# Gate and up of one layer as seven block products instead of eight, and its down products in four sections instead of three

## The chip, the core and the metric

The kernel runs on one core of a Trainium2 chip. The metric is the device time of one execution in microseconds (us), the median of several runs. The core has five engines with queues of their own: TensorE (PE, matrix products; its weight loads are PEld), VectorE (DVE), ScalarE (ACT), GpSimd (POOL) and SyncE (SP, which here issues nearly all DMAs). They meet only through semaphores. SBUF is the on-chip memory with 128 partitions, PSUM the eight banks into which TensorE writes.

## The reference

Two layers of a hybrid encoder over 512 prompt tokens and 64 sample tokens (576 in all, D_MODEL 1024, D_FF 2816). Each layer is a token mixer (a state-space scan and a windowed attention), then a feed-forward block. What the change touches is the feed-forward block of the second layer:

```
h2 = rmsnorm(x, norm_ffn_g) * (1 + sc_f) + sh_f          # [576, 1024]
gate, up = jnp.split(h2 @ w_gate_up, 2, axis=-1)          # w_gate_up [1024, 2 * 2816]
x = x + gt_f * ((jax.nn.silu(gate) * up) @ w_down)        # w_down [2816, 1024]
```

## The kernel before

Activations lie transposed: channels on the partitions, the 576 tokens along the row, in two halves of 288 (`H0`, `H1`; `HALF` = 288). Every fp32 product is made of three fp32r products: an operand is split into a rounded part (`hi`) and the rest (`lo`), and TensorE adds hi*hi, lo*hi and hi*lo in PSUM. `split` does this with one ScalarE cast (`S.copy` into `whi`) and one subtraction (`wlo`) on VectorE or, where the granule's `eng` is `G`, on GpSimd.

Weights come in granules (`Gran`) of 8 x 128 rows by 128 columns, 512 KB, through a ring of four raw buffers (`RAWB`). A granule becomes two `whi` and two `wlo` tiles of [128, 4, 128], in rings of four each (`WB`). `loads` issues the DMA of the next granule once an earlier one has been split; `advance` splits the granules of the present job, and after the job's first half one granule more. A `Job` is 128 output columns: 8 blocks of 128 input channels, 3 matmuls each, once per token half, thus 48 matmuls of 128 x 288. After each half `evac` takes the sum from PSUM.

The feed-forward block runs over 22 column blocks f of 128. For each there is a gate job and an up job (`gu_evac`: tanh, SiLU, product with up, split into `ah`, `al`). The blocks go in sections of 8, 8 and 6; after a section come eight down jobs that use its `ah`, `al` and add into x (`x_add`). Layer 1's first three blocks are done by halves (`by_halves`): six half jobs on the first 288 tokens, then the same six, with their weights loaded again, on the second. This covers the norm: `Norm.apply` for the second half is a side generator ("nf1") which `pump` steps between halves, and which is drained before the second six begin. `Norm.part` handles 256 channels of one half (`k2` = 0 to 3): scale, shift, cast into `hh`, rest into `hl`.

All matmuls of these jobs stand in `mm3` (L278 to L280). Granules of the mixer, and those done by halves, put the subtraction of `split` on GpSimd; the rest of layer 1's feed-forward block has `eng` unset, so VectorE does it (L167). The order of instructions on each engine is made by the framework's scheduler from the program's order, and is then fixed: an engine runs its queue strictly in order.

Of the kernel before, what the change touches and what calls it, by code (L numbers as in the profile page):

```python
# [19 lines left out]
TOK = SEQ + DEC  # L20
# [31 lines left out]
def hybrid_trunk(ctx: ExitStack, tc: tile.TileContext, I, O):  # L52
# [117 lines left out]
    class Gran:  # L170
# [16 lines left out]
        def split(self):  # L187
# [49 lines left out]
    def advance(upto):  # L237

        while gpos["split"] < min(upto, len(grans)):
            loads()  # L240
            g = grans[gpos["split"]]
            for _ in g.split():
                pass
            gpos["split"] += 1
            if not isinstance(g, Raw):
                gpos["rel"] += 1
            loads()
# [34 lines left out]
    class Job:  # L282
# [323 lines left out]
    class Norm:  # L606


        def __init__(self, l, which, xb):
            self.l, self.b = l, 0 if which == "mix" else 3  # L610
            self.xb = xb
            self.y = [None, None]
            self.ss = None

        def alloc(self):
# [36 lines left out]
        def part(self, half, k2, src, fast):  # L652
# [44 lines left out]
    def layer(l, nrm, jobs):  # L697
# [755 lines left out]
        n2 = lambda k, half: st["n2"].rhs(k, half)  # L1453
        secs = ((0, 8), (8, 8), (16, 6))

        def gu_evac(f, f0):
            def evac(m, half, ps):
                h = HS[half]
                if m == 0:
                    t = st["gate", f, half] = w2("gate", [128, HALF])  # L1460
                    act(t, ps[:, 0:HALF], ACTF.Tanh, scale=0.5)
                    stt(t, t, 1.0, ps[:, 0:HALF], ALU.add, ALU.mult)
                    return
                if f == f0 and half == 0:
# [44 lines left out]
        for sec, (f0, nf) in enumerate(secs):  # L1509
            gu_jobs = lambda fs: [job1(Gran(I["w_gate_up"][l], 0, 8, m * DFF + f * 128, 128), m, n2, gu_evac(f, f0))  # L1510
                                  for f in fs for m in range(2)]
# [167 lines left out]
```

## Time and profile before

| | |
|---|---|
| median of 3 runs | 2574.4 us (2573.2 to 2575.51) |
| the profiled execution | 2575.55 us, its span 2573.8 us, so 1.75 us lie around the span |
| busy over the span | PE 98%, PEld 93%, DVE 63%, ACT 41%, POOL 41% |
| granted TensorE clock | 0.991 of full speed, mean over the span |
| layer 1's feed-forward block | from about 2137 us to the end |

Busy time is a share over the whole span; the stages differ. POOL's row of the 40 slices is 0 in the last six, from about 2188 us on: there VectorE makes the `wlo`.

### The profile page before, as it was taken

To read this page: it belongs to the slowest core of one execution; us is meant where nothing else is said; L and a number is where in the kernel's file an instruction comes from. 1 tells how busy PE (TensorE), PEld (TensorE's weight loads), DVE (VectorE), ACT (ScalarE), POOL (GpSimd) and SP (SyncE) were. 2 spreads that over 40 slices of the span, in tenths; PEclk is the share of its full clock that TensorE was granted. 3 is DMA by queue.
4 is the path that set the end of the run, shared out by engine and by line. 5 is a ranking of instruction groups with operands and counts; after the bars stand their busy time and mean duration, and the time that the engine had idled before them with its cause. 6 is when DMAs were issued, how large, how long until landed. Compare 5 with 4: busy or idle time off the path is not lost.

```text
span 2573.8 us, 49262 instructions
## 1 busy us (share of the span) xinstructions
PE 2520.1 (98%) x19609; PEld 2395.0 (93%) x19609; DVE 1611.3 (63%) x2991; ACT 1060.8 (41%) x2383; POOL 1054.9 (41%) x968
## 2 busy tenths in 40 slices
PE   7999999999999999999999999999999999999999
PEld 6888999999889999999988899999988999999999
DVE  4598677745765765565686995956467656444443
ACT  3445454443453532222355454543444445323222
POOL 3444455343225754444586464553422266000000
PEclk8999999999999999999999999999999999999999
DMA  8555523243224555545574333332321255222222
GB/s 230 159 157 157 152 86 99 81 103 76 54 58 118 162 166 155 166 140 154 158 183 128 91 95 103 93 102 79 94 70 50 78 147 150 83 83 83 83 79 75
DMA packets 464107, 294.34 MB, mean 114 GB/s; under 512 B 69093, under 2 KB 446405, under 8 KB 463877
## 3 DMA queue, kind: packets, MB, share of 16 engines
q1 hardware_dynamic: 463876, 291.18, 39.4%
q8 instruction: 155, 2.54, 0.4%
q14 instruction: 76, 0.61, 0.1%
HBM read 276.98 MB, written 13.16 MB: 113 GB/s over the span
## 4 chain that ended last, share of the span: by engine, by line
PE 74%; DVE 14%; issue 3%; POOL 2%; ACT 1%; DMA 1%; ACTq 0%; SPq 0%; POOLq 0%; DVEq 0%
PE dps L278 22%; PE dps L280 22%; PE dps L279 21%; DVE cv L153 3%; DVE xT L153 2%; DVE seg L156 1%; PE sc L1213 1%; POOL wlo L167 1%; PE pv L1276 1%; PE pT L1260 1%; PE sp L926 1%; DVE hl L156 1%; PE yp L916 1%; DVE bc L156 1%; DVE S L156 1%
## 5 line engine op out<-in xcount | busy, mean ns | idle before, releaser
L167 POOL TENSOR_TENSOR wlo<-raw,whi 128x512 fp32r<-128x512 f32 (+1 forms) x632 | 896.8, 1427 | 857.6 <-ACT whi L166 743.7
L278 PE MATMUL dps<-hh,whi 128*128 128x288 f32 x3536 | 1055.8, 299 | 4.0 <-ACT hh L672 2.8
L279 PE MATMUL dps<-hh,wlo 128*128 128x288 f32 x3536 | 1050.0, 297 | 2.4 <-POOL wlo L167 2.4
L280 PE MATMUL dps<-hl,whi 128*128 128x288 f32 x3536 | 1049.7, 297 | 1.2 <-DVE hl L156 1.1
L166 ACT CAST whi<-raw 128x512 fp32r<-128x512 f32 (+1 forms) x762 | 462.0, 610 | 555.6 <-PE dps L280 433.2
L278 PEld LDWEIGHTS dps<-hh,whi 128*128 128x128 f32 x3536 | 665.1, 188 | 26.1 <-issue 16.4
L279 PEld LDWEIGHTS dps<-hh,wlo 128*128 128x128 f32 x3536 | 666.3, 188 | 11.3 <-issue 5.4
L280 PEld LDWEIGHTS dps<-hl,whi 128*128 128x128 f32 x3536 | 665.9, 188 | 8.1 <-issue 5.3
L279 PE MATMUL dps<-ah,wlo 128*128 128x288 f32 x704 | 210.8, 299 | 3.7 <-POOL wlo L167 3.7
L278 PE MATMUL dps<-ah,whi 128*128 128x288 f32 x704 | 207.8, 296 | 3.1 <-ACT ah L166 2.6
L280 PE MATMUL dps<-al,whi 128*128 128x288 f32 x704 | 208.3, 296 | 0.0
L153 DVE SCALAR_TENSOR_TENSOR ada_acc<-araw,csl,ada_acc 128x1024 f32<-128x1024 f32 x98 | 153.2, 1602 | 70.1 <-DMA araw<-in_ada_w_dram 66.2
L153 DVE SCALAR_TENSOR_TENSOR cv<-u,colB,cv 128x579 f32<-128x579 f32 x144 | 146.1, 1014 | 30.3 <-ACT cv L159 22.9
L278 PE MATMUL dps<-yh,whi 128*128 128x288 f32 x512 | 153.0, 299 | 1.2 <-ACT u L808 1.1
L280 PE MATMUL dps<-yl,whi 128*128 128x288 f32 x512 | 153.8, 300 | 0.0
L279 PE MATMUL dps<-yh,wlo 128*128 128x288 f32 x512 | 151.7, 296 | 0.0
L279 PEld LDWEIGHTS dps<-ah,wlo 128*128 128x128 f32 x704 | 132.8, 189 | 6.7 <-POOL wlo L167 5.5
L167 DVE TENSOR_TENSOR wlo<-raw,whi 128x512 fp32r<-128x512 f32 (+1 forms) x124 | 83.7, 675 | 87.2 <-ACT whi L166 85.8
L278 PEld LDWEIGHTS dps<-ah,whi 128*128 128x128 f32 x704 | 132.6, 189 | 4.0 <-ACT ah L166 2.8
L280 PEld LDWEIGHTS dps<-al,whi 128*128 128x128 f32 x704 | 132.8, 189 | 0.2 <-DVE al L167 0.2
L278 PEld LDWEIGHTS dps<-yh,whi 128*128 128x128 f32 x512 | 97.3, 190 | 4.5 <-issue 1.9
L280 PEld LDWEIGHTS dps<-yl,whi 128*128 128x128 f32 x512 | 97.3, 190 | 2.0 <-issue 1.8
(326 smaller groups left out, 3863.6 us busy)
## 6 DMA issues: line engine op xcount, KB each, us to landing
raw<-in_w_in_dram SPq DMA_DIRECT2D x119, 512.0 KB
raw<-in_w_gate_up_dram SPq DMA_DIRECT2D x100, 512.0 KB
araw<-in_ada_w_dram SPq DMA_DIRECT2D x56, 512.0 KB
bc<-ac_dr SPq DMA_DIRECT2D x32, 512.0 KB
raw<-in_w_br_ssm_dram SPq DMA_DIRECT2D x32, 512.0 KB
raw<-in_w_out_dram SPq DMA_DIRECT2D x32, 512.0 KB
raw<-in_w_down_dram SPq DMA_DIRECT2D x32, 512.0 KB
raw<-in_ada_w_dram SPq DMA_DIRECT2D x24, 512.0 KB
```

The lines of the kernel that those rows point to most:

```text
L153: V.scalar_tensor_tensor(out=out, in0=in0, scalar=scalar, in1=in1, op0=op0, op1=op1)
L156: V.tensor_tensor(out=out, in0=in0, in1=in1, op=op)
L166: S.copy(out=hi, in_=src)
L167: (eng or V).tensor_tensor(out=lo, in0=src, in1=f32(hi), op=ALU.subtract)
L278: T.matmul(ps, lhsT=wh, rhs=rh, start=a == 0, stop=False)
L279: T.matmul(ps, lhsT=wl, rhs=rh, start=False, stop=False)
L280: T.matmul(ps, lhsT=wh, rhs=rl, start=False, stop=a == nk - 1)
L916: T.matmul(yp[64 * r:64 * r + 64, m * 128:m * 128 + Lc], lhsT=xd[0:Lc, h, :], rhs=seg[0:Lc, h, 0:Lc], start=m == 0, stop=sprev is None and ...
L926: T.matmul(sp, lhsT=bn[0:Lc, i], rhs=xw[j], start=a == 0, stop=a == 2)
L1213: T.matmul(ps[:, pi * 192:pi * 192 + nk], lhsT=q[64 * r:64 * r + 64, pi, ch].rearrange("p h q -> p (h q)"), rhs=kT[64 * r:64 * r + 64, t, ...
L1260: T.transpose(ps[0:n, pi * 128:(pi + 1) * 128], s[:, r, pi, 64 * pi * (half is not None):][:, 0:n], ident)
L1276: T.matmul(ps[64 * r:64 * r + 64, 0:256], lhsT=vn[0:n, vt, cols[r]], rhs=pts[r][0:n, 0:256], start=True, stop=half is None)
```

## The change

In layer 1 (`WIDE`) the 19 column blocks after the first three become `PairJob`s. A pair job makes gate and up of one column block together. The product is cut into halves three ways: input channels (k 0 to 3 and 4 to 7), tokens (`H0`, `H1`) and gate/up. That would be eight block products of 12 matmuls. Seven are made instead, of sums of blocks on both sides, and their results are added again afterwards (Winograd's form of Strassen's scheme).

- Weights: four sums per pair on GpSimd (`PairGran.step`), from which, with three plain blocks, seven pairs of `whi` and `wlo` are split. For two of the seven (`POOL_LO`: steps 4 and 5) GpSimd also makes `wlo`.
- Activations: four sums `T1` to `T4` of the norm's quarters, made once in `Norm.combine`, called at the end of `part` in the second half; they too are split.
- Results: four PSUM banks per pair, from the two pools in turn; `pair_evac` adds them on VectorE.
- Both raw buffers of a pair are released after its step 6.
- `a` takes three blocks with hi and lo together; the sections are 4, 6, 6, 6, so eight down jobs more, with the same number of matmuls in all.

The core of the diff:

```diff
+    POOL_LO = (4, 5)
+    WIDE = (1,)
+    class PairGran(Gran):
+        def step(self, s):
+            p = self.pair
+            g, u = p["gate"], p["up"]
+            if s == 0:
+                p["s12"], p["s34"] = (w4("ws", [128, 2, 4, 128]) for _ in range(2))
+                p["hi"], p["lo"] = [], []
...
+            if s == 1:
+                G.tensor_tensor(out=s1, in0=u.block(1, 0), in1=u.block(1, 1), op=ALU.add)
+                G.tensor_tensor(out=s2, in0=s1, in1=g.block(0, 0), op=ALU.subtract)
+            if s == 2:
+                G.tensor_tensor(out=s3, in0=g.block(0, 0), in1=u.block(1, 0), op=ALU.subtract)
+            if s == 6:
+                G.tensor_tensor(out=s4, in0=g.block(0, 1), in1=s2, op=ALU.subtract)
+            x = (g.block(0, 0), s2, s3, s1, g.block(0, 1), u.block(1, 1), s4)[s]
...
+            split(hi, lo, x, G if s in POOL_LO else V)
...
+            if s == 6:
+                g.raw = u.raw = None
+                gpos["rel"] += 2
+                loads()
+    class PairJob:
+        def run(self):
+            nm, p, u = self.nrm(), self.gr[0].pair, self.gr[1]
+            a, b, cc, d = [(sps if self.i % 2 else dps)("wps")[:, 0:HALF] for _ in range(4)]
+            def product(s, ps, first):
+                rh, rl = nm.wino[("11", "T2", "T3", "T1", "21", "T4", "22")[s]]
+                wh, wl = p["hi"][s], p["lo"][s]
+                for k in range(4):
...
+            ev = self.evac(a, b, cc, d)
+            product(0, a, True)
+            u.step(4)
+            product(1, b, True)
+            next(ev)
+            u.step(5)
+            product(2, cc, True)
+            next(ev)
+            u.step(6)
+            product(3, d, True)
+            next(ev)
+            product(4, a, False)
+            next(ev)
+            yield
+            product(5, cc, False)
+            next(ev)
+            product(6, d, False)
+            next(ev)
+            yield
@@ Norm.part
+            if self.wide and half:
+                self.combine(k2, t)
+        def combine(self, k2, t):
...
+            def less(x, nm, eng, sign=1):
+                o = w4("tw", [128, 2, HALF])
+                h, lo = parts(nm)
+                if sign == 1:
+                    eng.tensor_tensor(out=o, in0=x, in1=h, op=ALU.subtract)
+                    eng.tensor_tensor(out=o, in0=o, in1=lo, op=ALU.subtract)
...
+            if k2 < 2:
+                put("T1", less(t, "11", G), V)
+                return
+            t2 = less(t, "T1", V)
+            put("T2", t2, V)
+            put("T3", less(t, "12", G), G)
+            put("T4", less(t2, "21", V, -1), V)
@@ layer
-        secs = ((0, 8), (8, 8), (16, 6))
+        secs = ((0, 4), (4, 6), (10, 6), (16, 6)) if wide else ((0, 8), (8, 8), (16, 6))
+        def pair_evac(f, f0, nf):
+            def evac(a, b, cc, d):
+                u2 = w2("u2", [128, HALF])
+                S.copy(out=u2, in_=a)
+                tt(u2, u2, b, ALU.add)
...
+                tt(u3, u2, cc, ALU.add)
...
+                tt(u3, u3, d, ALU.add)
...
+                act(g0, a, ACTF.Tanh, scale=0.5)
+                stt(g0, g0, 1.0, a, ALU.add, ALU.mult)
...
+                tt(t, u2, cc, ALU.add)
+                tt(t, t, g0, ALU.mult)
+                split(hi[:, H0], lo[:, H0], t)
...
+                tt(u2, u2, d, ALU.add)
+                act(g1, u2, ACTF.Tanh, scale=0.5)
+                stt(g1, g1, 1.0, u2, ALU.add, ALU.mult)
+                tt(g1, g1, u3, ALU.mult)
+                split(hi[:, H1], lo[:, H1], g1)
+            if wide:
+                jobs += [PairJob(I["w_gate_up"][l], f, lambda: st["n2"], pair_evac(f, f0, nf), f)
+                         for f in range(f0 + lead, f0 + nf)]
```

What the change does to the queues is seen at three places. The first is GpSimd's queue while the first three blocks of layer 1 are done by halves. Before, it holds only the `wlo` subtractions of the half jobs, two per job; from the row with `raw_25435` (the fifth half job of the first half) on they are:

```order
L167 TENSOR_TENSOR wlo_25620<-raw_25435,whi_25619 128x512
L167 TENSOR_TENSOR wlo_25624<-raw_25435,whi_25623 128x512
L167 TENSOR_TENSOR wlo_25658<-raw_25485,whi_25657 128x512
L167 TENSOR_TENSOR wlo_25662<-raw_25485,whi_25661 128x512
L167 TENSOR_TENSOR wlo_25696<-raw_25535,whi_25695 128x512
L167 TENSOR_TENSOR wlo_25700<-raw_25535,whi_25699 128x512
```

In the changed program the subtractions of `combine` (`tw`, lines 796 and 797) stand between the same ones:

```order
L169 TENSOR_TENSOR wlo_25663<-raw_25435,whi_25662 128x512
L796 TENSOR_TENSOR tw_25454<-nt2_25441,hh_25047 128x576
L169 TENSOR_TENSOR wlo_25667<-raw_25435,whi_25666 128x512
L796 TENSOR_TENSOR tw_25505<-nt2_25497,hh_25047 128x576
L797 TENSOR_TENSOR tw_25454<-tw_25454,hl_25049 128x576
L169 TENSOR_TENSOR wlo_25701<-raw_25495,whi_25700 128x512
L169 TENSOR_TENSOR wlo_25705<-raw_25495,whi_25704 128x512
L797 TENSOR_TENSOR tw_25505<-tw_25505,hl_25049 128x576
```

So the two `wlo` of the sixth half job (`raw_25485` before, `raw_25495` now) stand behind three subtractions that wait for the norm's second half.

The second place is GpSimd's queue in the pair jobs of a section. Before it has nothing there: its last rows are those of the half jobs, and then the program's end:

```order
L167 TENSOR_TENSOR wlo_25886<-raw_25741,whi_25885 128x512
L167 TENSOR_TENSOR wlo_25890<-raw_25741,whi_25889 128x512
L1672 UNCONDITIONAL_BRANCH
L1672 ISA
```

Now, with A to F for the six pairs of the section from f = 4 on, it holds in turn the four sums of one pair (`ws`; here C, raw 26504 and 26506), the two `wlo` of the pair before (B, raw 26340 and 26379), the sums of D, the two `wlo` of C:

```order
L227 TENSOR_TENSOR ws_26686<-raw_26506 128x512
L230 TENSOR_TENSOR ws_26687<-raw_26504,raw_26506 128x512
L228 TENSOR_TENSOR ws_26686<-ws_26686,raw_26504 128x512
L232 TENSOR_TENSOR ws_26687<-raw_26504,ws_26686 128x512
L169 TENSOR_TENSOR wlo_26613<-raw_26340,whi_26612 128x512
L169 TENSOR_TENSOR wlo_26632<-raw_26379,whi_26631 128x512
L227 TENSOR_TENSOR ws_26833<-raw_26656 128x512
L230 TENSOR_TENSOR ws_26834<-raw_26654,raw_26656 128x512
L228 TENSOR_TENSOR ws_26833<-ws_26833,raw_26654 128x512
L232 TENSOR_TENSOR ws_26834<-raw_26654,ws_26833 128x512
L169 TENSOR_TENSOR wlo_26760<-raw_26504,whi_26759 128x512
L169 TENSOR_TENSOR wlo_26779<-raw_26506,whi_26778 128x512
```

The raw buffers of D (26654, 26656) are those of B; they can be loaded only when B's two `wlo` have been made, and D's sums stand before the `wlo` of C.

The third place is VectorE's queue in the same pair. Before, a gate and an up job (a column block) bring ten instructions, here those from one gate's product on:

```order
L153 SCALAR_TENSOR_TENSOR gate_26090<-gate_26090,dps_26065 128x288
L167 TENSOR_TENSOR wlo_26160<-raw_25931,whi_26159 128x512
L153 SCALAR_TENSOR_TENSOR gate_26128<-gate_26128,dps_26103 128x288
L167 TENSOR_TENSOR wlo_26164<-raw_25931,whi_26163 128x512
L156 TENSOR_TENSOR gate_26090<-gate_26090,dps_26131 128x288
L167 TENSOR_TENSOR al_25523<-gate_26090,ah_25521 128x288
```

Now a pair brings sixteen, here pair B's from its last `wlo` (step 6, 26651) on, mixed with the first four `wlo` of C (steps 0 to 3: 26689, 26695, 26736, 26740):

```order
L169 TENSOR_TENSOR wlo_26651<-ws_26540,whi_26650 128x512
L158 TENSOR_TENSOR u3_26647<-u3_26647,wps_26599 128x288
L169 TENSOR_TENSOR wlo_26689<-raw_26504,whi_26688 128x512
L155 SCALAR_TENSOR_TENSOR gate_26683<-gate_26683,wps_26596 128x288
L169 TENSOR_TENSOR wlo_26695<-ws_26686,whi_26694 128x512
L158 TENSOR_TENSOR nt_26710<-u2_26628,wps_26598 128x288
L158 TENSOR_TENSOR nt_26710<-nt_26710,gate_26683 128x288
L169 TENSOR_TENSOR wlo_26736<-ws_26687,whi_26735 128x512
L158 TENSOR_TENSOR u2_26628<-u2_26628,wps_26599 128x288
L169 TENSOR_TENSOR a_26533<-nt_26710,a_26533 128x288
L169 TENSOR_TENSOR wlo_26740<-ws_26686,whi_26739 128x512
L155 SCALAR_TENSOR_TENSOR gate_26728<-gate_26728,u2_26628 128x288
```

The `wlo` of C's fourth product stands behind the first half of B's results, and behind it follow the steps of B's second half.

## Rows read from the trace of the kernel before

**Rows 1.** The page: the span, the engines' busy times, and two rows of the 40 equal slices (64.3 us each; a digit is tenths busy).

```profile
span 2573.8 us, 49262 instructions
PE 2520.1 (98%) x19609; PEld 2395.0 (93%) x19609; DVE 1611.3 (63%) x2991; ACT 1060.8 (41%) x2383; POOL 1054.9 (41%) x968
...
PE   7999999999999999999999999999999999999999
...
POOL 3444455343225754444586464553422266000000
```

**Rows 2.** The window view of 2180 to 2560 us, most of layer 1's feed-forward block: length, busy us (instructions) of each engine, granted clock, DMA share and GB/s.

```profile
2180.00:2560.00 380.00, 380.00 (x2874) 380.00 (x2873) 159.54 (x306) 107.15 (x211) 0.00 (x0) 1.00 0.29 84
```

**Rows 3.** VectorE's timeline around the first ordinary column block (f = 3): start us, us, instruction, and in brackets the idle time before it and what ended that.

```profile
2183.20 0.46 DVE L156 TENSOR_TENSOR gate<-gate,dps 128x288 f32<-128x288 f32 x1 [0.21 <-PE dps L280]
...
2186.80 0.46 DVE L153 SCALAR_TENSOR_TENSOR gate<-gate,dps 128x288 f32<-128x288 f32 x1 [1.83 <-ACT gate L159]
...
2199.52 0.46 DVE L153 SCALAR_TENSOR_TENSOR gate<-gate,dps 128x288 f32<-128x288 f32 x1 [1.84 <-ACT gate L159]
...
2212.24 0.46 DVE L153 SCALAR_TENSOR_TENSOR gate<-gate,dps 128x288 f32<-128x288 f32 x1 [1.83 <-ACT gate L159]
```

**Rows 4.** Groups of instructions from 2190 us to the end, by shape: count, busy us, mean ns of one, idle time before.

```profile
L167 DVE TENSOR_TENSOR wlo<-raw,whi 128x512 fp32r<-128x512 f32 x103 | 71.3, 692 | 73.7 <-ACT whi L166 72.5
L167 DVE TENSOR_TENSOR al<-gate,ah 128x288 fp32r<-128x288 f32 x38 | 17.3, 455 | 9.5 <-ACT ah L166 9.5
L156 DVE TENSOR_TENSOR gate<-gate,dps 128x288 f32<-128x288 f32 x38 | 17.3, 454 | 33.2 <-PE dps L280 33.2
...
L153 DVE SCALAR_TENSOR_TENSOR x<-dps,mod,x 128x288 f32<-128x288 f32 x24 | 12.4, 518 | 39.8 <-PE dps L280 39.8
...
L166 ACT CAST whi<-raw 128x512 fp32r<-128x512 f32 x103 | 63.8, 620 | 133.1 <-PE dps L280 125.5 <-issue 7.6
L166 ACT CAST ah<-gate 128x288 fp32r<-128x288 f32 x38 | 16.4, 433 | 51.9 <-DVE gate L156 51.9
L159 ACT ACTIVATE gate<-dps 128x288 f32<-128x288 f32 x36 | 14.8, 412 | 56.2 <-PE dps L280 56.2
```

**Rows 5.** GpSimd's timeline before and in the first three column blocks (an entry x3 is three instructions one behind the other).

```profile
2130.06 4.83 POOL L167 TENSOR_TENSOR wlo<-raw,whi 128x512 fp32r<-128x512 f32 x3 [0.77 <-ACT whi L166]
2136.82 7.98 POOL L167 TENSOR_TENSOR wlo<-raw,whi 128x512 fp32r<-128x512 f32 x6 [1.94 <-ACT whi L166]
...
2151.57 1.30 POOL L167 TENSOR_TENSOR wlo<-raw,whi 128x512 fp32r<-128x512 f32 x1 [0.23 <-ACT whi L166]
...
2171.15 1.29 POOL L167 TENSOR_TENSOR wlo<-raw,whi 128x512 fp32r<-128x512 f32 x1 [1.07 <-ACT whi L166]
```

**Rows 6.** VectorE's timeline in the same stretch.

```profile
2130.23 1.74 DVE L156 TENSOR_TENSOR hl<-nt,hh 128x576 fp32r<-128x576 f32 x1
...
2132.09 1.65 DVE L156 TENSOR_TENSOR hl<-nt,hh 128x576 fp32r<-128x576 f32 x1
...
2141.95 0.45 DVE L153 SCALAR_TENSOR_TENSOR gate<-gate,dps 128x288 f32<-128x288 f32 x1 [0.80 <-ACT gate L159]
...
2153.20 0.74 DVE L156 TENSOR_TENSOR hl<-nt,hh 128x576 fp32r<-128x576 f32 x1
...
2171.44 1.32 DVE L167 TENSOR_TENSOR al<-gate,ah 128x288 fp32r<-128x288 f32 x1 [0.59 <-ACT ah L166]
```

**Rows 7.** ScalarE's casts of the norm's second half (`hh`, the first two of four) in the same stretch.

```profile
2150.31 0.67 ACT L672 CAST hh<-nt 128x576 fp32r<-128x576 f32 x1
...
2153.01 0.67 ACT L672 CAST hh<-nt 128x576 fp32r<-128x576 f32 x1 [1.51 <-DVE nt L670]
```

**Rows 8.** The view of the tile `raw` from 2200 to 2260 us, its row on gate and up loads issued by SP (ns min/median/max of the issue, first and last start).

```profile
L185 SPq DMA_DIRECT2D raw<-in_w_gate_up_dram x2: 367/368/368, 2203.9 to 2210.1; - x2
```

**Rows 9.** The window view in half microseconds behind the first of those loads; the last two columns are the DMA engines' busy share and GB/s.

```profile
2204.50:2205.00 0.50, 0.50 (x6) 0.50 (x6) 0.00 (x0) 0.00 (x0) 0.00 (x0) 1.00 0.01 2
2205.00:2205.50 0.50, 0.50 (x6) 0.50 (x5) 0.07 (x1) 0.00 (x0) 0.00 (x0) 1.00 0.51 138
...
2206.50:2207.00 0.50, 0.50 (x6) 0.50 (x5) 0.35 (x1) 0.00 (x0) 0.00 (x0) 1.00 0.90 269
2207.00:2207.50 0.50, 0.50 (x5) 0.50 (x5) 0.00 (x0) 0.42 (x1) 0.00 (x0) 1.00 0.10 30
```

**Rows 10.** TensorE's timeline at idle times that were ended by other engines.

```profile
2138.16 0.40 PE L279 MATMUL dps<-hh,wlo 128*128 128x288 f32 x1 [0.73 <-POOL wlo L167]
...
2160.55 0.40 PE L278 MATMUL dps<-hh,whi 128*128 128x288 f32 x1 [0.56 <-ACT whi L166]
...
2163.27 0.61 PE L278 MATMUL dps<-hh,whi 128*128 128x288 f32 x1 [1.41 <-ACT hh L672]
...
896.16 0.45 PE L278 MATMUL dps<-hh,whi 128*128 128x288 f32 x1 [1.43 <-ACT hh L672]
```

**Rows 11.** The window view behind two of them; the column before the last two is the granted clock.

```profile
894.00:896.00 2.00, 0.73 (x5) 0.49 (x4) 1.71 (x3) 0.56 (x1) 0.99 (x1) 1.00 0.40 103
...
2162.00:2164.00 2.00, 0.73 (x2) 0.50 (x2) 1.57 (x5) 1.19 (x2) 0.29 (x2) 0.68 0.85 252
2164.00:2166.00 2.00, 2.00 (x9) 1.94 (x9) 1.08 (x4) 1.52 (x4) 1.71 (x2) 0.50 0.03 7
...
2168.00:2170.00 2.00, 2.00 (x12) 2.00 (x11) 0.00 (x0) 0.62 (x1) 1.19 (x1) 0.62 0.41 110
```

More of the change, by code (lines that the diff above doesn't have):

```diff
@@ L199, in split, with __init__, block @@
             self.raw = None
+    class PairGran(Gran):
+        def __init__(self, w, c0, first=None):
+            super().__init__(w, 0, 8, c0, 128)
+            self.first = first
+            self.pair = first.pair if first else {}
+            self.pair["up" if first else "gate"] = self
+        def block(self, i, h):
+            return self.raw[:, 4 * h:4 * h + 4]
+        def step(self, s):
[4 more added lines that the diff above has]
+                p["hi"], p["lo"] = [], []
+            s1, s2 = p["s12"][:, 0], p["s12"][:, 1]
+            s3, s4 = p["s34"][:, 0], p["s34"][:, 1]
+            if s == 1:
[6 more added lines that the diff above has]
+            x = (g.block(0, 0), s2, s3, s1, g.block(0, 1), u.block(1, 1), s4)[s]
+            hi = wp.tile([128, 4, 128], F32R, tag="whi", bufs=WB, name="whi")
+            lo = wp.tile([128, 4, 128], F32R, tag="wlo", bufs=WB, name="wlo")
+            split(hi, lo, x, G if s in POOL_LO else V)
+            p["hi"].append(hi)
+            p["lo"].append(lo)
+            if s == 6:
+                g.raw = u.raw = None
+                gpos["rel"] += 2
+                loads()
+        def split(self):
+            for s in ((2, 3) if self.first else (0, 1)):
+                self.step(s)
+                yield
     class Raw(Gran):
@@ L244, in advance @@
             gpos["split"] += 1
-            if not isinstance(g, Raw):
+            if not isinstance(g, (Raw, PairGran)):
                 gpos["rel"] += 1
@@ L613, in __init__ @@
             self.ss = None
+            self.wide = which == "ffn" and l in WIDE
+            self.wino = None
         def alloc(self):
@@ L1463, in evac @@
                     return
-                if f == f0 and half == 0:
-                    st["ah"] = [blk("ah", [128, 4, TOK], F32R) for _ in range(2)]
-                    st["al"] = [blk("al", [128, 4, TOK], F32R) for _ in range(2)]
+                if half == 0:
+                    a_alloc(f, f0, nf)
                 t = st.pop(("gate", f, half))
                 tt(t, t, ps[:, 0:HALF], ALU.mult)
-                j = f - f0
-                hi = st["ah"][j // 4][:, j % 4, HS[half]]
-                split(hi, st["al"][j // 4][:, j % 4, HS[half]], t)
+                hi, lo = (x[:, HS[half]] for x in a_parts(f, f0))
+                split(hi, lo, t)
                 mark[0] = f32(hi[:, 0:1])
@@ L1516, in layer @@
                 gj[2 * lead].pre = lambda: drain("nf1")
-            jobs += gj + gu_jobs(range(f0 + lead, f0 + nf))
-            dn_jobs = lambda: [job1(Gran(I["w_down"][l], f0, nf, m * 128, 128), m, pair_rhs("a"), dn_evac(sec), nk=nf)
+            jobs += gj
+            if wide:
+                jobs += [PairJob(I["w_gate_up"][l], f, lambda: st["n2"], pair_evac(f, f0, nf), f)
+                         for f in range(f0 + lead, f0 + nf)]
+                if lead:
+                    jobs[-1].pre = lambda: drain("nf1")
+            else:
+                jobs += gu_jobs(range(f0 + lead, f0 + nf))
+            dn_jobs = lambda: [job1(Gran(I["w_down"][l], f0, nf, m * 128, 128), m, a_rhs, dn_evac(sec), nk=nf)
                                for m in range(8)]
-            jobs += by_halves(dn_jobs) if sec == 2 and l + 1 < DEPTH else dn_jobs()
+            jobs += by_halves(dn_jobs) if sec == len(secs) - 1 and l + 1 < DEPTH else dn_jobs()
         if l == 0:
```

68 lines of the change are left out of this document (65 added, 3 removed).

## The prediction

> **What bounds the kernel now.** First the page: TensorE is busy for 2520.1 of 2573.8 us, and GpSimd has nothing to do from about 2188 us on [rows 1]. Then the window view of the stage that changes: over 380 us TensorE has no idle time and runs 2874 matmuls, 0.132 us each, while VectorE is busy for 42% and ScalarE for 28% [rows 2]. So a matmul taken away here is worth 0.132 us as long as nothing else becomes late. A column block has 96 of them, 12.7 us, which VectorE's timeline shows too: the same step of the gate comes at 2186.80, 2199.52 and 2212.24 [rows 3]. The question is what the new work on GpSimd and VectorE makes late.
>
> **What is removed.** 19 pairs lose 12 matmuls each: 228 x 0.132 = 30.1 us. A pair then needs 84 x 0.132 = 11.1 us, a product of 12 about 1.6 us. The eight additional down jobs change no count of matmuls; their 24 updates of x (at most 0.52 us each [rows 4]) lie beside products of 3.2 us or more per job, with VectorE otherwise busy for under 1 us per job. If that cover were gone they would cost at most 12 us together; I take zero. ScalarE gets seven casts of 0.62, two of 0.43 and three passes of about 0.41 per pair [rows 4], 6.4 us of 11.1: hidden, but in order with the others, which matters below.
>
> **GpSimd in a pair.** Six instructions of 128 x 512: two `wlo`, as the rows of before have them at 1.29 to 1.30 us alone [rows 5], and four sums, which the trace does not show. They have the same size and two SBUF operands; I bound them by 1.29 and by 1.61 (three `wlo` in 4.83 us [rows 5]) and take 1.3, since what makes the difference is counted separately. That is 7.8 us of 11.1.
>
> **The load in GpSimd's loop.** D's sums need raw buffers that are free only after B's two `wlo`. A load issued at 2203.9 [rows 8] moves bytes from about 2205.0 to 2207.1 [rows 9]: 1.1 us until the first byte, 2.0 for 512 KB. A pair loads two, one behind the other, 4.9 us after the first of the two `wlo` at the earliest. GpSimd's loop is then 4.9 + 4 x 1.3 + 1.3 = 11.4 us, hardly longer than TensorE's 11.1. Alone it would cost about 1 us per section.
>
> **What VectorE and GpSimd do to each other.** An `hl` of 128 x 576 takes 0.74 us where GpSimd is idle (2153.20), but 1.74 and 1.65 us at 2130.23 and 2132.09, and an `al` of 128 x 288 takes 1.32 at 2171.44 instead of 0.455 [rows 4, 6]. Each of these began during a GpSimd `wlo` and ended 0.3 to 0.6 us after it (2171.15 + 1.29 = 2172.44; the `al` ended at 2172.76) [rows 5, 6]. GpSimd pays too: three `wlo` took 4.83 us rather than 3.9, with two `hl` between them, so about 0.45 us each. An operation that reads PSUM is not delayed: the gate step at 2141.95 took 0.45 us [rows 6] in the middle of six `wlo` without a gap [rows 5]. So VectorE instructions with two SBUF operands get one turn per GpSimd instruction. The Trainium skill (SBUF — State Buffer, Who interferes with whom) says that a VectorE instruction with two SBUF inputs and a GpSimd instruction that reads SBUF exclude each other for the whole instruction. The wait of VectorE agrees with it; GpSimd's 0.45 us is less than the 0.74 that it would have by this rule.
>
> A pair has ten such instructions on VectorE (five `wlo`, and in each half's results the multiplications and subtractions without PSUM) and six that read PSUM. I work through a section of six pairs A to F, 0 being where A's products begin. A and B's sums lie in the down jobs before. C's sums run from 8.5 to 14.6, while A's results are made; B's fifth block loses about 0.5 us, since its cast stands on ScalarE behind the cast of A's second half, whose multiplication has waited for a turn. B's products end at 22.9. D's loads are issued at 16.5 and 19.7, D's sums begin at 22.8. VectorE then has four instructions in a row that each wait for one sum (1.3 us plus 0.15 to 0.45): the product for B's first half ends at 24.3, C's `wlo` of step 2 at 26.0, a subtraction at 27.5, C's `wlo` of step 3 at 29.2. Product 3 of C could have begun at 22.9 + 3 x 1.6 = 27.7: **1.5 us late**. Then B's multiplication waits for GpSimd's `wlo` of step 4 (until 31.1), its cast ends at 31.6, the cast of step 5 behind it at 32.2, GpSimd's `wlo` at 33.6, where TensorE wanted it at 32.4: **1.2 us late**. D's and E's products meet the sums of E and F in the same way; F meets none. A section thus loses 0.5 + 3 x 2.7 = 8.6 us, three lose 25.8, and the first 1.5 more, because its shorter down jobs (24 matmuls rather than 36) leave A's and B's sums less room: 27.3 us.
>
> **The lead.** In the first three column blocks GpSimd gets ten operations of 128 x 576 for `combine`, by size 1.3 x 576/512 = 1.46 us, and VectorE fourteen. The sixth half job's first `wlo` ended at 2151.57 + 1.30 = 2152.9, about 1 us before TensorE came to it. Now it stands behind a subtraction that needs the `hh` cast ending at 2151.0, a `wlo`, a subtraction that needs the cast ending at 2153.7 [rows 7], and one more: 2151.0 + 1.46 + 1.3 + 1.46 + 1.46 + 1.3 = 2158.0. Part of this wait replaces one: TensorE waited 0.56 and 1.41 us for this norm anyway, and ran at half clock behind it (0.50 at 2164, back at full speed by 2169.7) [rows 10, 11]. From 2158.0 to the last `wlo` of the lead GpSimd has 13 `wlo` (16.9 us), seven operations of `combine` (10.2), two sums (2.6) and some 14 turns of VectorE's at about 0.25 (3.5): 2191.2. TensorE does 12 matmuls more, waits for the second sum, its cast and its rest (1.3 + 0.62 + 0.69), and then six products (9.6): the first pair ends at about 2204. Before, the same block began at 2183.2 [rows 3] and ended 12.7 later, at 2195.9. That is 8.1 us later although this pair has saved 1.6: 9.7 us.
>
> **Sum.** -30.1 + 27.3 + 9.7 = +6.9 us on the profiled execution's 2575.55: 2582.5. The median lay 1.15 below that execution, so **2581 us**; with the terms' ends (turns of 0.15 or 0.45 us, sums of 1.29 or 1.6) 2571 to 2591. About 0.2% (5.1 us) is what can be told from no change here.
>
> **Rivals.**
> - *The turns don't collide* (faster). Then GpSimd's loop of 11.4 us is all there is, 3 us over three sections, and the lead costs some 7.6: -30.1 + 3 + 7.6 = -19.5, so 2555. It speaks for it that VectorE has only 8 to 9 us of work in 11.1, and could do it while GpSimd waits for loads; against it, that the rows show a full wait at each collision, and that the sums begin just when a pair's last results come. With two of the four collisions avoided (1.3 of 2.7 us) it is 2569. The point from which it decides: C's `wlo` of step 3 ready less than 0.5 us after its product could begin.
> - *Whole instructions exclude each other.* A pair then takes the sum of both engines' shares: 7.8 + 5 x 0.69 + 5 x 0.455 = 13.5 us where before had 12.7. 18 pairs lose 14 us in all, the lead's 8.1 stays: 2597. It is what the rule cited above would make of it.
> - *The clock falls at the late products.* An idle 1.41 us with 0.56 shortly before it was followed by about 6.5 us at 0.50, the lower of the two levels; 1.43 us at 896.16 was not, nor 0.73 [rows 10, 11]. At half clock a matmul takes 0.24 us, so some 27 matmuls cost 2.9 us, of which the second wait takes back 1.2. If it happens in all nine late pairs, 9 x 1.7 = 15 us on top of the forecast: 2596 and more.
>
> **How the numbers follow.** Forecast 0.44, turns that don't collide 0.30, whole exclusion 0.16, the clock 0.10. The range leaves out the fastest third of the second case (0.10) and what exceeds 2602 (about 0.08): 2553 to 2602. Faster than 2569.3: 0.29, nearly all of the second case. Between 2569.3 and 2579.5: some two fifths of the forecast's share and a little of the second, 0.19. Slower: 0.52.
>
> **What would show it.** Per section, pairs A and F near 11.1 us, C, D and E near 13.9, by the distance of the same step on VectorE. VectorE's `wlo` of 128 x 512 at a mean of 1.1 to 1.4 us rather than 0.69; GpSimd's sums at 1.3 to 1.7. TensorE waiting for VectorE's `wlo` ahead of the fourth product and for GpSimd's ahead of the sixth. The first pair ending near 2204. In the down jobs no idle time. Wrong it would be if VectorE's `wlo` stay near 0.7 us: then the second rival holds; if GpSimd's loop is longer than its instructions and the load, a wait that I have not seen; or if the first pair ends before 2198.

## The result and the profile after

The changed kernel takes 2600.51 us (median of four runs, 2599.31 to 2604.75) where the kernel before took 2574.95 in the same session (2573.2 to 2575.88): a ratio of 1.0103 with a 95% interval of 1.0086 to 1.0121. It is 25.6 us slower; the forecast was 2581, 6 us slower, with a range of 2553 to 2602. The profiled execution took 2604.75 us, and its layer 1 stage begins 3.9 us later than in the trace of before: GpSimd's run of six `wlo` starts at 2140.75 (before 2136.82, [rows 5]). Those 3.9 us lie ahead of the change.

The page after, to be held against [rows 1]:

```profile
span 2603.0 us, 49408 instructions
PE 2508.9 (96%) x19381; PEld 2378.2 (91%) x19381; DVE 1737.2 (67%) x3159; ACT 1107.6 (43%) x2483; POOL 1244.4 (48%) x1092
...
PE   7999999999999999999999999999999997999989
...
POOL 3445455343225754544675555544422378436260
```

TensorE has exactly the 228 matmuls less (19609 to 19381) but only 11.2 us less of busy time, and the rows of the 40 slices show it no longer full at the end, where GpSimd has got work. The window view tells the rest: two stretches of the lead (the first three blocks and the first pair), then the pairs of the three sections, then two stretches of down products (columns as in [rows 2]):

```profile
2142.00:2180.00 38.00, 29.05 (x201) 27.90 (x201) 32.69 (x42) 17.44 (x34) 31.93 (x24) 0.91 0.39 112
2180.00:2214.00 34.00, 27.79 (x175) 26.16 (x176) 22.35 (x29) 14.50 (x29) 27.09 (x18) 0.90 0.21 63
...
2260.00:2315.00 55.00, 48.84 (x339) 48.13 (x340) 42.49 (x64) 23.51 (x48) 32.32 (x22) 0.94 0.28 80
2315.00:2366.00 51.00, 51.00 (x387) 51.00 (x386) 28.82 (x58) 15.17 (x30) 14.09 (x10) 1.00 0.33 97
2366.00:2433.00 67.00, 57.76 (x417) 56.74 (x416) 51.57 (x80) 29.62 (x60) 38.43 (x26) 0.97 0.25 71
2433.00:2483.00 50.00, 50.00 (x380) 50.00 (x379) 28.72 (x57) 14.73 (x29) 13.84 (x10) 1.00 0.33 95
2483.00:2552.00 69.00, 60.78 (x416) 59.34 (x415) 55.22 (x80) 29.37 (x60) 38.95 (x26) 0.93 0.24 69
```

In the down products TensorE has no gap. In the three stretches of pairs it is idle for 6.2 + 9.2 + 8.2 = 23.6 us, and its 1172 matmuls take 167.4 us where at 0.132 they would take 154.7: 12.7 us more, most of it at the lower clock (the granted clock of the three stretches is 0.94, 0.97 and 0.93 in the mean). What it waits for, from 2130 to 2610 us (total us, times, longest):

```profile
PE wps L371 <- POOL wlo L169: 25.3, 14, 3.1
PE dps L326 <- ACT whi L168: 13.4, 6, 5.7
PE dps L327 <- POOL wlo L169: 1.1, 2, 0.7
PE wps L369 <- ACT whi L168: 0.8, 2, 0.6
PE wps L371 <- DVE wlo L169: 0.3, 1, 0.3
```

Two waits, then: in the pairs (`wps`) GpSimd's `wlo`, in the lead (`dps`) ScalarE's `whi`. To size both, I cut the stage of each trace in two: the **lead** goes from the start of GpSimd's run of six `wlo` to TensorE's first matmul with `a` and a `wlo`, where the down products begin, the **rest** from there to the end of the span. The two rows of after, and then those of a run with the new sections but ordinary jobs (e2 below), the plain form of the same split:

```profile
2140.75 7.97 POOL L169 TENSOR_TENSOR wlo<-raw,whi 128x512 fp32r<-128x512 f32 x6 [1.94 <-ACT whi L168]
2214.79 0.29 PE L327 MATMUL dps<-a,wlo 128*128 128x288 f32 x1
```

```profile
2143.22 7.96 POOL L169 TENSOR_TENSOR wlo<-raw,whi 128x512 fp32r<-128x512 f32 x6 [1.94 <-ACT whi L168]
2201.34 0.29 PE L327 MATMUL dps<-a,wlo 128*128 128x288 f32 x1
```

Lead, rest and pair are those of the one profiled execution of each kernel, the last column is of all its runs. The pair length is the distance of the same tanh on ScalarE, as a mean over the five distances in each section; an ordinary block has 12.72 [rows 3], and 84 matmuls at 0.132 take 11.1.

| kernel | lead | rest | pair | time, ratio to before |
|---|---|---|---|---|
| e2, ordinary jobs in the new sections | 58.1 | 378.1 | - | 1.0006 |
| changed kernel | 74.0 | 388.2 | 13.70 | 1.0103 |
| e1, no sums of the activations | 58.5 | 387.5 | 13.65 | 1.0033 |
| e3, sums of the weights without a load | 77.8 | 368.7 | 12.14 | 1.0045 |
| e4, all `wlo` of the pairs on VectorE | 74.0 | 365.0 | 12.17 | 1.0015 |
| e6, results that stay in PSUM | 74.8 | 381.5 | 13.24 | 1.0075 |
| e7, e3 and e6 together | 77.1 | 351.1 | 11.15 | 0.998 |
| e5, sums of the activations later in the program | 72.1 | 387.7 | 13.63 | 1.0098 |
| e5b, these sums held late | 57.9 | 389.3 | 13.25 | 1.0047 |
| e8, e4 and e6 and e5 | 72.3 | 349.9 | 11.16 | 0.9956 |
| e9, e4 and e6 and e5b | 57.8 | 358.2 | 11.2 | 0.9909 |

The changed kernel against e2: the lead is 15.9 us longer, and the rest, which should have become 18 x 12 x 0.132 = 28.5 us shorter, is 10.1 longer. What a run's total differs by beyond its stage lies ahead of the change: the six `wlo` begin anywhere from 2131.86 (e9) to 2143.22 us (e2), so it is the stages that are compared here.

Two pair lengths can be told apart only if they differ by more than about half a microsecond. The changed kernel, e5 and e5b have the same pairs in the last two sections, and there the means are 13.56 and 13.98, 13.29 and 13.32, 13.05 and 13.07.

### The profile page after: what moved, and what is told of

Its sections match the earlier page's. It is cut to its first block, busy times and chain, and to the rows that moved or that the text cites. A ratio compares the mean times of both kernels' runs of the same rounds, so it can differ in the third digit from the quotient of the medians.

```text
span 2603.0 us, 49408 instructions
## 1 busy us (share of the span) xinstructions
PE 2508.9 (96%) x19381; PEld 2378.2 (91%) x19381; DVE 1737.2 (67%) x3159; ACT 1107.6 (43%) x2483; POOL 1244.4 (48%) x1092
## 4 chain that ended last, share of the span: by engine, by line
PE 70%; DVE 15%; POOL 5%; DMA 5%; issue 3%; ACT 2%; SPq 0%; ACTq 0%; POOLq 0%; DVEq 0%
PE dps L326 19%; PE dps L328 19%; PE dps L327 19%; DVE cv L155 3%; POOL wlo L169 3%; DMA raw<-in_w_gate_up_dram 2%; DVE xT L155 2%; DVE seg L158 1%; PE sc L1353 1%; PE wps L371 1%; PE pv L1416 1%; PE wps L372 1%; PE wps L369 1%; POOL ws L228 1%; PE pT L1400 1%
## 5 line engine op out<-in xcount | busy, mean ns | idle before, releaser
L326 PE MATMUL dps<-hh,whi 128*128 128x288 f32 x2928 | 878.6, 301 | 15.5 <-ACT whi L168 14.0
L327 PE MATMUL dps<-hh,wlo 128*128 128x288 f32 x2928 | 872.1, 298 | 2.8 <-POOL wlo L169 2.8
L328 PE MATMUL dps<-hl,whi 128*128 128x288 f32 x2928 | 871.4, 298 | 1.1 <-DVE hl L158 1.1
L168 ACT CAST whi<-raw 128x512 fp32r<-128x512 f32 (+2 forms) x759 | 453.7, 601 | 510.3 <-PE dps L328 366.7
L326 PEld LDWEIGHTS dps<-hh,whi 128*128 128x128 f32 x2928 | 552.3, 189 | 38.6 <-issue 16.8
L327 PEld LDWEIGHTS dps<-hh,wlo 128*128 128x128 f32 x2928 | 553.0, 189 | 12.0 <-POOL wlo L169 5.5
L328 PEld LDWEIGHTS dps<-hl,whi 128*128 128x128 f32 x2928 | 552.8, 189 | 7.7 <-issue 5.3
L155 DVE SCALAR_TENSOR_TENSOR ada_acc<-araw,csl,ada_acc 128x1024 f32<-128x1024 f32 x98 | 152.4, 1593 | 72.1 <-DMA araw<-in_ada_w_dram 72.1
L327 PE MATMUL dps<-ah,wlo 128*128 128x288 f32 x352 | 105.6, 300 | 4.1 <-POOL wlo L169 4.1
L327 PE MATMUL dps<-a,wlo 128*128 128x288 f32 x352 | 104.4, 298 | 0.0
L326 PE MATMUL dps<-a,whi 128*128 128x288 f32 x352 | 103.1, 295 | 0.0
L328 PE MATMUL dps<-a,whi 128*128 128x288 f32 x352 | 102.8, 295 | 0.0
```

The costliest lines, as they stand in the source:

```text
L155: V.scalar_tensor_tensor(out=out, in0=in0, scalar=scalar, in1=in1, op0=op0, op1=op1)
L168: S.copy(out=hi, in_=src)
L326: T.matmul(ps, lhsT=wh, rhs=rh, start=a == 0, stop=False)
L327: T.matmul(ps, lhsT=wl, rhs=rh, start=False, stop=False)
L328: T.matmul(ps, lhsT=wh, rhs=rl, start=False, stop=a == nk - 1)
```

## The experiments

**e1: the lead without the sums of the activations.** `T1` to `T4` are the plain quarters, so `combine` does nothing; this leaves the sums out.

```diff
+                for n, q in (("T1", "11"), ("T2", "12"), ("T3", "21"), ("T4", "22")):
+                    self.wino[n] = self.wino[q]
+            return
```

> The sums of activations are left out (T1 to T4 are the plain quarters, so the numbers computed in layer 1 are others); pairs, sections and all the rest stay. If the lead's loss comes from combine's ten GpSimd and fourteen VectorE operations in the queues, the 15 us by which the first pair ended later in the changed kernel's trace (2141.1 to 2214.9 against 2137.1 to 2195.9) go, and the pair's own saving of 1.6 us shows: about 2584 us. If the lead is slow because of the first pair's own weights and sums, it stays above 2595.

Measured 2583.21 (ratio 1.0033, 1.0021 to 1.0046). The lead falls from 74.0 to 58.5, TensorE's waits in it to those that the kernel before had too (1.4, 0.7 and 0.5 us, [rows 10]) and 0.8; the pairs stay. So `combine` costs 15.5 us, and the pairs are slow without it.

**e2: the new sections alone.** Ordinary jobs for all blocks.

```diff
-            if wide:
+            if wide and False:
```

> Ordinary gate and up jobs throughout, no combine, only the sections 4, 6, 6, 6. The prediction put the eight additional down jobs at nothing: 2575 us, within 1.5. If their updates of x or their smaller granules are not hidden, up to 12 us more: 2580 to 2587.

Measured 2576.55 (1.0006, 0.9996 to 1.0016). The eight additional down jobs cost nothing that can be told.

**e3: the sums of the weights without their load.** They read two tiles that lie in SBUF all along, so they wait for no DMA; this computes other numbers with the same work.

```diff
-                G.tensor_tensor(out=s1, in0=u.block(1, 0), in1=u.block(1, 1), op=ALU.add)
+                G.tensor_tensor(out=s1, in0=r0, in1=r1, op=ALU.add)
```

(and s2, s3, s4 likewise)

> GpSimd's four sums per pair read two tiles that lie in SBUF all the time instead of the raw weights (so the products are others); their number, size and two SBUF operands stay, and with them the turns with VectorE, but no sum waits for a load any more. If the load that stands ahead of the next pair's subtractions in GpSimd's queue is what makes a pair 14 us long (5.1 us idle per pair in the trace), a pair comes to 11.1 to 12 us and the time to about 2567. If the turns alone make it, as the prediction had it, pairs C to E stay near 13.9 and the time at 2592 to 2600.

Measured 2588.3 (1.0045, 1.0029 to 1.0061), between the two theories. Pairs are 12.14 in the mean, inside a section 12.5, one like the other:

```profile
2375.29 0.41 ACT L161 ACTIVATE gate<-wps 128x288 f32<-128x288 f32 x1 [0.98 <-PE wps L373]
2387.60 0.41 ACT L161 ACTIVATE gate<-wps 128x288 f32<-128x288 f32 x1 [0.97 <-PE wps L373]
2400.14 0.41 ACT L161 ACTIVATE gate<-wps 128x288 f32<-128x288 f32 x1 [0.97 <-PE wps L373]
```

The wait for GpSimd's `wlo` has gone, and what TensorE now waits for in the pairs is a result that VectorE hasn't taken out of PSUM:

```profile
PE wps L370 <- DVE u L158: 11.5, 10, 1.2
PE wps L370 <- ACT whi L168: 2.8, 3, 1.0
```

So both theories hold a part: the load lengthens a pair by 1.56, and under it lies a second bound, 1.0 above the matmuls. That bound is VectorE, which with its waits for turns is busy for 58.35 of the 61 us from 2364 to 2425. (The lead is 3.8 us longer than that of the changed kernel, probably because the first sums, which wait for no load, move up into it: the first stands 52.0 us behind the start of the six `wlo`, in the changed kernel 57.1.)

**e4: no `wlo` of the pairs on GpSimd.**

```diff
-    POOL_LO = (4, 5)
+    POOL_LO = ()
```

> All seven subtractions of a pair on VectorE; GpSimd has only the four sums, with nothing behind them in its queue that a product waits for soon. By the load theory a pair falls to 11.5 to 12.5 us, 18 pairs save 20 to 35 us: 2568 to 2580. By the turns theory VectorE then has 9.8 us of its own work and four or more full waits of 1.3 us, so some 14 us per pair: 2598 or more.

Measured 2578.02 (1.0015, 1.0006 to 1.0024), pairs of 12.17. Nothing that releases a raw buffer stands behind GpSimd's sums now, and the loop is open. VectorE has two `wlo` more and is not worse for it: its `wlo` have a mean of 0.85 to 0.90 us. What TensorE still waits for in the pairs is VectorE (`u` 4.8 us in all, `wlo` 4.2). The turns theory alone (2598 or more) is refuted.

**e6: results that stay in PSUM.** The changed kernel; each operation of `pair_evac` after the first ones writes into the bank that it reads, so that it has at most one operand in SBUF.

```diff
-                tt(t, u2, cc, ALU.add)
-                tt(t, t, g0, ALU.mult)
-                split(hi[:, H0], lo[:, H0], t)
+                tt(cc, u2, cc, ALU.add)
+                tt(cc, g0, cc, ALU.mult)
+                split(hi[:, H0], lo[:, H0], cc)
```

(and the second half in `d`)

> Only the pair's results change: each operation of them writes back into PSUM and reads at most one operand from SBUF, so VectorE has five instructions per pair with two SBUF operands instead of ten. GpSimd's sums still wait for the loads. Load theory (GpSimd's loop of about 14.3 us is the bound, and the turns add little to it): pairs stay at 13 to 14.5, 2593 to 2600. Turns theory (VectorE's late results and blocks are the bound): pairs of 12 to 12.7, 2575 to 2585.

Measured 2591.99 (1.0075, 1.0058 to 1.0092), pairs of 13.24; 1 us below the load theory's 2593 to 2600. The length by itself can't be told from that of the unchanged pairs (13.05 to 13.98 above); what counts is that the pairs stay long with the turns of the results gone. VectorE's operations on results run at 0.45 us again (`a<-wps,a` 452 ns, `wps<-u,wps` 462), and GpSimd still stands waiting for its load:

```profile
2381.13 2.94 POOL L169 TENSOR_TENSOR wlo<-raw,whi 128x512 fp32r<-128x512 f32 x2
2388.89 1.40 POOL L227 TENSOR_TENSOR ws<-raw 128x512 f32<-128x512 f32 x1 [4.82 <-DMA raw<-in_w_gate_up_dram]
2390.25 1.75 POOL L230 TENSOR_TENSOR ws<-raw 128x512 f32<-128x512 f32 x1
2391.97 1.29 POOL L228 TENSOR_TENSOR ws<-ws,raw 128x512 f32<-128x512 f32 x1
2393.33 1.31 POOL L232 TENSOR_TENSOR ws<-raw,ws 128x512 f32<-128x512 f32 x1
2394.59 2.98 POOL L169 TENSOR_TENSOR wlo<-raw,whi 128x512 fp32r<-128x512 f32 x2
```

**e7: e3's resident sums and e6's results together.**

> The results by PSUM and, at the same time, the four sums made from two resident tiles, so that they wait for no load (other numbers come out; work, sizes and order are the same). If the wait for the loads and the turns of the results are all that lengthens a pair: pairs of 11.1 to 11.6 us and about 2560 to 2565, the lead being unchanged. If a third cause holds the pairs (VectorE's blocks waiting for turns, ScalarE's casts in order, the clock): 12 us or more per pair, 2572 or more.

Measured 2567.14 (0.998, 0.9971 to 0.999). Pairs are 11.15 in each of the three sections, and behind the first pair TensorE waits for nothing but 0.3 us at the program's end. The load and the turns of the results are thus all that lengthened the pairs: 13.70 with both, 13.24 and 12.14 with one of them, 11.15 with neither. VectorE's `wlo` still take turns (mean 1.01 and 1.19 us) and cost nothing. The time is 2 us above what I expected, by the longer lead that e3 has too.

**e5 and e5b: the sums of the activations elsewhere.** In both the fourth column block is an ordinary one (18 pairs), and `combine` is a side generator that starts there and takes `t` anew from hi + lo.

> Only the sums of the activations are moved: out of the lead, into the ordinary jobs and the eight down jobs of the first section, whose fourth column block is an ordinary one (18 pairs rather than 19, so 1.6 us are given back). Theory (the lead's cost is GpSimd's and VectorE's queues there, and it is hidden anywhere else): 2600.5 - 17 + 1.6 = about 2585, pairs as in the changed kernel, 13 to 15 us, since GpSimd's loop is untouched. Rival (the sums cost the same wherever they stand, since they take turns with the down jobs' updates of x): 2597 or more.

Measured 2596.15 (1.0098, 1.0077 to 1.0119): a miss, but of the edit: the lead is still 72.1. The scheduler had put the sums back into the lead, as GpSimd's timeline shows:

```profile
2152.76 1.44 POOL L806 TENSOR_TENSOR tw<-hh,hl 128x576 f32<-128x576 f32 x1 [1.16 <-DVE hl L158]
```

e5b ties each first sum to the lead's last result by a copy of one column into its buffer, and has the subtractions for `T2` and `T3` on GpSimd, the rests on VectorE, so not quite the same work on each engine:

```diff
+            G.tensor_copy(out=t[:, 0, 0:1], in_=self.hold)
             G.tensor_tensor(out=t, in0=h, in1=lo, op=ALU.add)
```

> The changed kernel with only its sums of the activations moved, and held there by the same dependency; the fourth column block is an ordinary one, and the pairs are as in the changed kernel. Theory (the lead's 17 us are the queues of GpSimd and VectorE there, and the same sums are hidden later): 2599 - 17 + 1.6 = about 2584 (2580 to 2588). Rival (the sums cost the same wherever they stand): 2593 or more.

Measured 2587.17 (1.0047, 1.0031 to 1.0062), near the upper end of what the theory gave. The lead is 57.9, its waits those of before and 0.2. But the sums aren't free where they stand now: the first begins 46.8 us behind the start of the six `wlo` (2179.78 against 2133.02) instead of 13.5, and the rest is 1.1 us longer than in the changed kernel although its 15 pair distances are 0.45 shorter each. As an estimate they cost about 8 us there (1.1 + 6.7), half of 15.5. The shorter pairs are no merit of the edit as far as is shown, since the same pairs differ by as much between runs; but e9 against e8, with equal pairs, gives 8.3 for the same place.

**e8: all rests on VectorE (e4), results in PSUM (e6), late sums without the hold (e5).**

> All seven rests of the weights on VectorE (GpSimd keeps the four sums and no work behind the raw buffers' release), results by PSUM, the sums of the activations in the first section. VectorE then has some 7 x 0.69 + 11 x 0.455 = 9.8 us of a pair's 11.1. Theory: 18 pairs of 11.1 to 11.8 us where before had 12.7: 2574.9 - 18 x 1.3 = about 2551 (2547 to 2560). Rival (VectorE, 9.8 us plus turns with four sums, becomes the bound at 12 us or more): 2562 to 2572.

Measured 2561.75 (0.9956, 0.9941 to 0.9971), 1.8 us above the theory's range and at the lower end of the rival's (2562), but the pairs decide against the rival's 12 us or more: they are at 11.16, and behind the lead TensorE doesn't wait, so the rest is 28.2 us shorter than in e2, all that the matmuls are worth. The lead is still 14.2 longer, since these sums stand where those of e5 do.

**e9: e8 with e5b's hold.**

> As the version with all rests on VectorE, results by PSUM and late sums of the activations, but now the late place is held by a dependency: before each first sum GpSimd copies one column of the lead's last result into the sum's buffer, so that nothing of it can be put ahead of that result. Of 16 sums on GpSimd (23 us by size) and 12 operations on VectorE all stand beside the fourth, ordinary column block (12.7 us) and eight down jobs (26 us). Theory: the lead is then that of the kernel before, the pairs stay at 11.2: 2573.1 - 18 x 1.5 = 2546, with a little for the first pair 2545 to 2553. Rival (the stall comes back in the first section, where updates of x stand behind the sums on VectorE, or at the first pair, whose sums of the weights stand behind these on GpSimd): 2556 to 2562.

Measured 2551.32 (0.9909, 0.9891 to 0.9927) beside 2575.24 for the kernel before, 23.9 us less, and so less than both kernels. By its trace the stage is 21.1 us shorter than before (from the six `wlo` to the end 415.9, before 437.0). TensorE's waits from 2172 us on:

```profile
PE dps L327 <- DVE wlo L169: 1.8, 2, 1.6
PE dps L328 <- DVE a L169: 1.0, 1, 1.0
PE dps L326 <- DVE x L155: 0.7, 2, 0.4
PE wps L369 <- ACT gate L161: 0.4, 1, 0.4
PE wps L371 <- DVE wlo L169: 0.4, 1, 0.4
PE xo L1696 <- DVE x L155: 0.3, 1, 0.3
```

All but the last are of the first down jobs and the first pair, where VectorE has the late sums; with the lower clock behind them (0.83 from 2200 to 2210 us) they make most of the 8.3 us by which the rest is longer than that of e8.

## Why the prediction fell short

The direction was right and the range held the time, but the size was about a quarter of what was measured: +6.9 us by the sum, 25.6 in the medians. That the range reached up to 2602 was due to the two slow rivals, neither of which is what happened, so that it held the time was in part luck. With the terms as measured (against e2) the sum is -30.1 + 38.6 + 17.5 = 26.0; the stage of the two traces differs by 25.3. By terms:

**The matmuls (-30.1): right.** 228 fewer at the same 0.132; e8 gets back 28.2 us with 18 pairs (28.5 by the row). **The eight down jobs (0): right**, by e2.

**The load in GpSimd's loop (1 us per section): the step that failed most.** I had seen the loop, and called 11.4 us "hardly longer than TensorE's 11.1". GpSimd's timeline of after has it at 14.3 and 14.0:

```profile
2273.57 2.97 POOL L169 TENSOR_TENSOR wlo<-raw,whi 128x512 fp32r<-128x512 f32 x2
2281.69 1.65 POOL L227 TENSOR_TENSOR ws<-raw 128x512 f32<-128x512 f32 x1 [5.15 <-DMA raw<-in_w_gate_up_dram]
2283.30 1.51 POOL L230 TENSOR_TENSOR ws<-raw 128x512 f32<-128x512 f32 x1
2284.77 1.50 POOL L228 TENSOR_TENSOR ws<-ws,raw 128x512 f32<-128x512 f32 x1
2286.36 1.60 POOL L232 TENSOR_TENSOR ws<-raw,ws 128x512 f32<-128x512 f32 x1
2287.91 2.96 POOL L169 TENSOR_TENSOR wlo<-raw,whi 128x512 fp32r<-128x512 f32 x2
2296.02 1.30 POOL L227 TENSOR_TENSOR ws<-raw 128x512 f32<-128x512 f32 x1 [5.15 <-DMA raw<-in_w_gate_up_dram]
...
2301.92 2.96 POOL L169 TENSOR_TENSOR wlo<-raw,whi 128x512 fp32r<-128x512 f32 x2
```

From the first `wlo`'s end (2287.91 + 1.48 = 2289.4) to the sums there are 6.6 us, not 4.9 (by my own terms it would have been 1.1 + 2 x 2.0 = 5.1); the sums and one `wlo` take 7.4 to 7.7, not 6.5. The load's windows show where the 1.7 us lie (last column GB/s):

```profile
2290.50:2291.00 0.50, 0.50 (x4) 0.50 (x4) 0.00 (x0) 0.00 (x0) 0.37 (x1) 0.50 0.31 86
...
2292.00:2292.50 0.50, 0.50 (x4) 0.50 (x4) 0.00 (x0) 0.29 (x1) 0.00 (x0) 0.50 1.13 339
...
2294.50:2295.00 0.50, 0.50 (x6) 0.50 (x5) 0.44 (x1) 0.39 (x1) 0.00 (x0) 1.00 0.25 69
2295.00:2295.50 0.50, 0.50 (x6) 0.50 (x5) 0.47 (x3) 0.23 (x1) 0.00 (x0) 1.00 0.19 53
```

The bytes of both loads move from about 2290.6 to about 2295.3, 4.7 us rather than twice the 2.0 of [rows 9], with a thin tail; GpSimd starts 0.7 us behind the last of them, a delay that I had left out. And the loop closes, since the next pair's four sums stand ahead of this pair's two `wlo` in GpSimd's queue: a late load makes the sums late, these the `wlo`, these TensorE's fifth product (3.14 us idle at 2289.68) and the next release. What I had costed as 1 us per section is the largest bound of the pair. "If GpSimd's loop is longer than its instructions and the load" stood among the ways to be wrong; what I had too short was the load itself, by 1.7 us, and the instructions, by 0.9 to 1.2.

**The turns (27.3): seen rightly, placed wrongly.** VectorE's instructions with two SBUF operands wait where GpSimd is at work: its `wlo` are at 0.94 and 1.03 us in the mean (forecast 1.1 to 1.4), the multiplication of the second half, `gate<-gate,u`, at 0.98. Those that read PSUM stay at 0.45; GpSimd's sums are at 1.46 to 1.52 (1.3 to 1.7). But TensorE waits for VectorE's `wlo` just once, 0.3 us: the first of my two collisions does not happen, and the product that is late is the fifth, for GpSimd's `wlo`. The results of the first half, which I had put beside the sums, mostly run while GpSimd stands idle for its load (2276.5 to 2281.7 above). Their multiplication has two SBUF operands too, and takes 0.46 us (so too in the mean of all pairs), where that of the second half waits for a sum:

```profile
2279.42 0.46 DVE L158 TENSOR_TENSOR nt<-nt,gate 128x288 f32<-128x288 f32 x1
...
2282.22 1.43 DVE L158 TENSOR_TENSOR gate<-gate,u 128x288 f32<-128x288 f32 x1
```

By e3 the turns alone would cost 1.0 us per pair and by e6 the load alone 2.1; together it is 2.6, and whether the turns add that half microsecond to the load isn't shown, since the same pairs differ by as much between runs. The 18 pairs lose 38.6 us (28.5 saved, 10.1 longer), where I had 27.3. Those that I had as C to E take 13.1 to 15.5, forecast 13.9; the last of a section takes 11.1 to 12.5, forecast near 11.1.

**The lead (9.7): the right cause, the wrong queue.** By the cut above it is 15.9 net and 17.5 with the 1.6 that its pair saves; `combine` has 15.5 of it. The first pair, forecast to end near 2204, ends about 2214.8, or 2210.9 without the 3.9 us ahead of the stage. I walked GpSimd's queue, yet TensorE waits for `whi`: ScalarE's casts of weights stand in order behind its casts `hh` and `T`, and these wait for VectorE. ScalarE's timeline ahead of the longest wait (TensorE idle for 5.65 us until 2171.24):

```profile
2165.04 0.67 ACT L767 CAST hh<-nt 128x576 fp32r<-128x576 f32 x1 [3.60 <-DVE nt L765]
...
2170.00 0.67 ACT L767 CAST hh<-nt 128x576 fp32r<-128x576 f32 x1 [2.43 <-DVE nt L765]
2170.57 0.61 ACT L168 CAST whi<-raw 128x512 fp32r<-128x512 f32 x1
```

VectorE is late because the norm's own steps take turns too, which I hadn't counted. They are `TENSOR_SCALAR` instructions out of SBUF:

```profile
2163.54 1.41 DVE L765 TENSOR_SCALAR nt<-nt,mod 128x64 f32<-128x64 f32 x1
...
2169.60 0.30 DVE L765 TENSOR_SCALAR nt<-nt,mod 128x64 f32<-128x64 f32 x1
```

128 x 64 takes 0.30 us alone and up to 1.41 beside GpSimd, and the trace of before has one of 1.36 already (at 2159.56). The sums of `combine` fill GpSimd's gaps: of the eight such steps (128 x 64 or 128 x 224) from 2154 us on, seven take 1.25 us or more. The Trainium skill (SBUF — State Buffer, Who interferes with whom) names `tensor_scalar` among the operations that can hold the shared ports; these rows agree with it.

**The rivals.** That the turns don't collide came true by the sign that it named: TensorE's only wait for VectorE's `wlo` is 0.3 us, and VectorE does the first half's results while GpSimd waits for its load. Its time fell, as the loop is 14.0 to 14.3 us rather than 11.4, and with the load gone the turns still cost 1.0 us per pair (e3 against e7). That whole instructions exclude each other (13.5 us per pair) fell with e3: 12.14 with all the turns left. The lower clock is at work behind some of the waits. It adds some 10 us to TensorE's busy time in the pairs (the mean clocks above over their 55, 67 and 69 us; the rest of the 12.7 is there in e3 too, 2.7 us at a clock of 1.00, where no wait is over 1.2 us). But it isn't what makes the pairs long: in the second section the clock stays at 1.00 until 2420 us, and GpSimd's loop is no shorter there, 13.8, 14.4 and 14.5 us:

```profile
2388.37 3.41 POOL L169 TENSOR_TENSOR wlo<-raw,whi 128x512 fp32r<-128x512 f32 x2
...
2402.72 2.96 POOL L169 TENSOR_TENSOR wlo<-raw,whi 128x512 fp32r<-128x512 f32 x2
```

## What to carry to other kernels

When a producer sits in a ring (use, release, load, produce), work the whole loop out with the transfers as they run one behind the other and the delay behind the last byte, and hold it against the consumer's period: a loop near that period is the bound, and it is opened by taking the releasing work off the engine that waits for the load. Price added work in an in-order queue by who stands behind it, on each engine that it feeds and not on its own alone. Here 15.5 us went to about 8 by letting nearly the same operations begin 33 us later, and that took a real dependency, since the scheduler had put the ready work back where it was.

## What the runs showed of the hardware beyond that

- VectorE operations that write their result back into the PSUM bank that they read run at 0.45 us beside a busy GpSimd (e6: `wps<-u,wps` 462 ns, `a<-wps,a` 452), where the same steps of the second half on SBUF tiles took 0.80 to 0.98 (`a<-gate,a` 796 ns, `gate<-gate,u` 975; two instructions go by the last name, the other took 856).
- An idle time of 3.14 us was followed by 3.5 us at a granted clock of 0.50, the lower level, and one of 3.09 likewise; one of 2.82 (at 2404.49) was followed by full speed. So the length of the gap alone doesn't decide it: one of 2.65 (at 2508.03) and in e6 one of 2.02 (at 2282.24) were followed by 0.50 too, and in [rows 10, 11] 1.41 us behind another gap of 0.56 was enough. The runs don't settle what does.
